# Row sums of a 16384 x 1024 array: 16-row loads in halves from two DMA queues, three blocks of rows, one store more

## The chip, the cores and the metric

The kernel runs on one core of a Trainium2 chip. The metric is the device time of one execution in microseconds (us). Before the change the median of three runs is 160.99 us (160.79 to 161.18). From here on "us" always means device time or a time in the trace of one profiled execution, counted from the first instruction.

## What is computed

The input x is 32 x 512 x 1024 numbers in f32, 67.11 MB. The output is the sum over the last axis, 32 x 512 numbers in f32:

```python
def reference(x):                      # x: (32, 512, 1024) f32
    return np.sum(x, axis=-1).astype(np.float32)
```

Seen flat, these are 16,384 rows of 1,024 columns (4,096 bytes), each summed to one number. Nothing is used twice, so every byte of x crosses from HBM to the on-chip memory (SBUF) once.

## The kernel before

**Layout.** The rows are spread over the 128 partitions, 128 rows for each. The flat array is cut in two blocks. In the first, `x_a` (BODY = 113 rows per partition), partition p holds 113 consecutive rows, so neighbouring partitions start 113 x 4 KB apart in HBM. In the second, `x_z` (LAST = 15 rows per partition), they start 60 KB apart. A column of results, `res_a` with 113 and `res_z` with 15 numbers per partition, belongs to each block.

**Loads.** All loads go out from SyncE (SP in the profile), on its one DMA queue, from the list `loads` at L133. Each is a DMA over all 128 partitions and takes one contiguous stretch per partition: one row (`lead`, 4,096 bytes per partition); seven loads of 16 rows (65,536 bytes per partition) into three buffers `xt0` to `xt2` in turn; then the last block in pieces of 8, 4 and 2 rows (CUTS = 0, 8, 12, 14) into the next of these buffers; then the last row in two parts of 656 and 368 columns (CUT = 656) into `tail`. The first two loads are moved ahead of the start barrier (EARLY = 2). A load into a buffer in its second or third use waits for the VectorE instruction that read the buffer before (`wait_ge(vec, freed[b - BUFS])`). Such a load is issued some 41 us before it lands, with two others ahead of it, and all loads stand in one line.

**Sums.** VectorE (DVE) sums rows with `tensor_reduce` (L58), one instruction for all the rows of a load. ScalarE (ACT) sums single rows with an activation that accumulates (L69). VectorE alone does the lead row and the first six 16-row loads. Of the seventh, VectorE does 9 rows and ScalarE 7 (ACT_ROWS = 7). Of the 8-row piece each does 4, of the 4-row piece each 2, and of the 2-row piece VectorE one row by an add of its two halves with accumulation (L76) and ScalarE the other. The last row's two parts go through L76 one after the other; the second takes in the sum of the first, and waits on `vec` for it.

**Stores.** SP waits until the first part of the last row has landed and until both engines are done with the first block, and stores `res_a` (L137, 452 bytes per partition). Then it waits for all sums and stores `res_z` (L140, 60 bytes per partition). It then waits for the first store, clears semaphores (L144) and waits for the last store.

Of the kernel before, what the change touches and what calls it, by code (L numbers as in the profile page):

```python
# [6 lines left out]
COPY = mybir.ActivationFunctionType.Copy  # L7
X = mybir.AxisListType.X

LEAD = 1  # L10
G = 16
BODY = LEAD + 7 * G
LAST = 15
BUFS = 3
ACT_ROWS = 7
CUT = 656
CUTS = (0, 8, 12, 14)
EARLY = 2


def row_sums(nc, x: bass.AP, out: bass.AP):
    P = nc.NUM_PARTITIONS
    x_flat = x.flatten_outer_dims()
    R, D = x_flat.shape
    C = R // P
    assert R % P == 0 and C == BODY + LAST
    out_flat = out.rearrange("a (b c) -> (a b c)", c=1)

    def block(r0, n):
        x_b = x_flat[r0 : r0 + P * n].rearrange("(p c) d -> p (c d)", p=P)  # L30
        out_b = out_flat[r0 : r0 + P * n].rearrange("(p c) -> p c", p=P)
        return x_b, out_b

    x_a, out_a = block(0, BODY)
    x_z, out_z = block(P * BODY, LAST)

    def sbuf(name, n):
        return nc.alloc_sbuf_tensor(name, [P, n], F32)

    xt = [sbuf(f"xt{i}", G * D) for i in range(BUFS)]  # L40
    lead = sbuf("lead", LEAD * D)
    tail = sbuf("tail", D + 16)
    pairs = [sbuf(f"pairs{i}", D // 2) for i in range(3)]
    res_a = sbuf("res_a", BODY)
    res_z = sbuf("res_z", LAST)

    names = [f"slot{i}" for i in range(BUFS)] + ["first", "piece0", "piece1", "piece2", "tail0"]
    names += ["tail1", "vec", "act", "early_store", "store"]
    sems = {n: nc.alloc_semaphore(n) for n in names}
    slots = [sems[f"slot{i}"] for i in range(BUFS)]  # L50
    vec, act = sems["vec"], sems["act"]
    numbers = [s.num for s in sems.values()]
    assert numbers == list(range(numbers[0], numbers[0] + len(numbers)))

    count = {"vec": 0, "act": 0}

    def rows_dve(t, j, n, res, c):
        nc.vector.tensor_reduce(  # L58
            out=res[:, c : c + n],
            in_=t[:, j * D : (j + n) * D].rearrange("p (j d) -> p j d", d=D),  # L60
            axis=X,
            op=ADD,
        ).then_inc(vec, 1)
        count["vec"] += 1

    def rows_act(t, j, n, res, c):
        for i in range(n):
            v = t[:, (j + i) * D : (j + i + 1) * D]
            nc.scalar.activation(  # L69
                out=v, in_=v, func=COPY, accum_out=res[:, c + i : c + i + 1]  # L70
            ).then_inc(act, 1)
            count["act"] += 1

    def pairs_dve(t, a, b, acc, pairs):
        h = (a + b) // 2
        nc.vector.tensor_tensor_reduce(  # L76
            out=pairs[:, 0 : h - a], in0=t[:, a:h], in1=t[:, h:b], scale=1.0, scalar=0.0,
            op0=ADD, op1=ADD, accum_out=acc,
        ).then_inc(vec, 1)
        count["vec"] += 1  # L80

    n_bufs = (BODY - LEAD) // G


    freed = {}
    loads = [(0, lead[:, :], x_a[:, 0 : LEAD * D], sems["first"])]
    for b in range(n_bufs):
        c = LEAD + b * G
        loads.append((b, xt[b % BUFS][:, :], x_a[:, c * D : (c + G) * D], slots[b % BUFS]))
    last = xt[n_bufs % BUFS]  # L90
    for k, (i, j) in enumerate(zip(CUTS, CUTS[1:])):
        loads.append((n_bufs, last[:, i * D : j * D], x_z[:, i * D : j * D], sems[f"piece{k}"]))
    for k, (i, j, gap) in enumerate(((0, CUT, 0), (CUT, D, 16))):
        e = (LAST - 1) * D
        loads.append((0, tail[:, i + gap : j + gap], x_z[:, e + i : e + j], sems[f"tail{k}"]))


    nc.vector.memset(tail[:, CUT + 15 : CUT + 16], 0.0).then_inc(vec, 1)  # L98
    count["vec"] += 1
    nc.vector.wait_ge(sems["first"], 16)  # L100
    rows_dve(lead, 0, LEAD, res_a, 0)
    for b in range(n_bufs):
        a = ACT_ROWS if b == n_bufs - 1 else 0
        nc.vector.wait_ge(slots[b % BUFS], 16 * (b // BUFS + 1))
        rows_dve(xt[b % BUFS], 0, G - a, res_a, LEAD + b * G)
        freed[b] = count["vec"]
        if a:
            nc.scalar.wait_ge(slots[b % BUFS], 16 * (b // BUFS + 1))
            rows_act(xt[b % BUFS], G - a, a, res_a, LEAD + b * G + G - a)
    body_vec, body_act = count["vec"], count["act"]  # L110

    for k in range(2):
        i, j = CUTS[k], CUTS[k + 1]
        h = (j - i) // 2
        nc.vector.wait_ge(sems[f"piece{k}"], 16)
        rows_dve(last, i, h, res_z, i)
        nc.scalar.wait_ge(sems[f"piece{k}"], 16)
        rows_act(last, i + h, j - i - h, res_z, i + h)
    nc.scalar.wait_ge(sems["piece2"], 16)
    rows_act(last, 13, 1, res_z, 13)  # L120
    nc.vector.wait_ge(sems["piece2"], 16)
    pairs_dve(last, 12 * D, 13 * D, res_z[:, 12:13], pairs[2])
    nc.vector.wait_ge(sems["tail0"], 16)
    pairs_dve(tail, 0, CUT, tail[:, CUT + 14 : CUT + 15], pairs[0])
    nc.vector.wait_ge(sems["tail1"], 16)
    nc.vector.wait_ge(vec, count["vec"])  # L126
    pairs_dve(tail, CUT + 14, D + 16, res_z[:, 14:15], pairs[1])


    for b, dst, src, s in loads:  # L130
        if b >= BUFS:
            nc.sync.wait_ge(vec, freed[b - BUFS])
        nc.sync.dma_start(out=dst, in_=src).then_inc(s, 16)  # L133
    nc.sync.wait_ge(sems["tail0"], 16)
    nc.sync.wait_ge(vec, body_vec)
    nc.sync.wait_ge(act, body_act)
    nc.sync.dma_start(out=out_a, in_=res_a[:, :]).then_inc(sems["early_store"], 16)  # L137
    nc.sync.wait_ge(vec, count["vec"])
    nc.sync.wait_ge(act, count["act"])
    nc.sync.dma_start(out=out_z, in_=res_z[:, :]).then_inc(sems["store"], 16)  # L140


    nc.sync.wait_ge(sems["early_store"], 16)
    nc.sync.sem_clear(range(numbers[0], sems["store"].num))  # L144
    nc.sync.wait_ge(sems["store"], 16).then_inc(sems["store"], -16)


def kernel(tc: tile.TileContext, x: bass.AP, out: bass.AP):
    tc.close()
    tc.compile()  # L150
    nc = tc.nc
    row_sums(nc, x, out)

    sp = mybir.EngineType.SP
    fn = nc.m.functions[0]
    entry, body = None, None
    for blk in fn.blocks:
        ops = [i for i in blk.instructions if i.engine == sp]  # L160
        if entry is None:
            entry = blk
        elif any(i.opcode == "DMACopy" for i in ops):
            body = blk
            break
    code = list(body.instructions)
    loads = [i for i in code if i.engine == sp and i.opcode == "DMACopy"][:EARLY]
    for load in loads:
        assert not load.sync_info.on_wait
        code.remove(load)  # L170
    body.instructions = code
    code = list(entry.instructions)
    at = next(k for k, i in enumerate(code) if i.engine == sp and i.opcode == "Drain")
    code[at:at] = loads
    entry.instructions = code
# [29 lines left out]
```

## Time and profile before

The profile is that of one execution. Times in its rows are in us from the first instruction; "idle before <-releaser" is the time that an engine stood idle ahead of an instruction and what ended it.

| | before |
|---|---|
| time, median of 3 runs | 160.99 us (160.79 to 161.18) |
| span of the profiled execution, first to last instruction | 159.7 us |
| what the median has beyond that span | 1.3 us |
| VectorE busy | 122.6 us (77%), 17 instructions |
| ScalarE busy | 16.3 us (10%), 29 instructions |
| DMA queue of SP | 2160 packets, 67.18 MB, 97.8% of 16 engines' span |
| a 16-row reduce on VectorE | 17,222 ns |
| a row on ScalarE | 1,041 ns, then 187 ns to read the accumulator |

The trace also holds each packet that a DMA engine moved: its start, its time and its size. A packet here is one partition's stretch of one load. Each of the 16 engines moves 8 of them per load, one after the other, and then a 4-byte packet that raises the semaphore (9 ns):

| bytes | of | packets | median time | starts of the first and the last, us |
|---|---|---|---|---|
| 4,096 | lead row | 128 | 159 ns | 1.02, 2.91 |
| 65,536 | 16 rows | 896 | 2,420 ns | 2.65, 136.22 |
| 32,768 | 8 rows | 128 | 1,213 ns | 138.14, 147.10 |
| 16,384 | 4 rows | 128 | 611 ns | 147.82, 152.57 |
| 8,192 | 2 rows | 128 | 309 ns | 152.69, 155.33 |
| 2,624 | 656 columns | 128 | 105 ns | 155.15, 156.35 |
| 1,472 | 368 columns | 128 | 62 ns | 155.97, 156.87 |
| 452 | store of `res_a` | 128 | 26 ns | 157.81, 158.13 |
| 60 | store of `res_z` | 128 | 11 ns | 158.86, 159.05 |

A load has landed when the slowest of its 16 engines has raised the semaphore. The last landings, by the semaphore records, are at 139.02 (the seventh 16-row load), 148.73, 153.62, 156.11, 156.95 and 157.37 us (second part of the last row).

### The profile page before, as it was taken

To read this page: it belongs to the slowest core of one execution; us is meant where nothing else is said; L and a number is where in the kernel's file an instruction comes from. 1 tells how busy PE (TensorE), PEld (TensorE's weight loads), DVE (VectorE), ACT (ScalarE), POOL (GpSimd) and SP (SyncE) were. 2 spreads that over 40 slices of the span, in tenths; PEclk is the share of its full clock that TensorE was granted. 3 is DMA by queue.
4 is the path that set the end of the run, shared out by engine and by line. 5 is a ranking of instruction groups with operands and counts; after the bars stand their busy time and mean duration, and the time that the engine had idled before them with its cause. 6 is when DMAs were issued, how large, how long until landed. Compare 5 with 4: busy or idle time off the path is not lost.

```text
span 159.7 us, 105 instructions
## 1 busy us (share of the span) xinstructions
DVE 122.6 (77%) x17; ACT 16.3 (10%) x29; POOL 0.2 (0%) x4
## 2 busy tenths in 40 slices
DVE  1100029999499985999779996899949999499984
ACT  3000000000000000000000000000000000196783
POOL 0000000000000000000000000000000000000000
DMA  9969969979799699699699699699796996999993
GB/s 394 525 263 525 509 279 525 460 328 525 328 460 525 263 525 525 263 525 525 263 525 509 279 525 492 295 525 443 345 525 295 492 525 295 476 410 394 435 394 107
DMA packets 2160, 67.18 MB, mean 421 GB/s; under 512 B 496, under 2 KB 624, under 8 KB 880
## 3 DMA queue, kind: packets, MB, share of 16 engines
q1 hardware_dynamic: 2160, 67.18, 97.8%
HBM read 67.11 MB, written 0.07 MB: 421 GB/s over the span
## 4 chain that ended last, share of the span: by engine, by line
DMA 75%; DVE 22%; SPq 1%; issue 0%; DVEq 0%
DMA xt<-in_x_dram 51%; DMA tail<-in_x_dram 24%; DVE res_a L58 22%; SPq L133 1%; DVE pairs L76 1%; DVEq L126 0%; DVE tail L76 0%; DVE res_z L76 0%
## 5 line engine op out<-in xcount | busy, mean ns | idle before, releaser
L58 DVE TENSOR_REDUCE res_a<-xt 128x16 f32<-128x16384 f32 (+1 forms) x7 | 113.1, 16155 | 31.0 <-DMA xt<-in_x_dram 31.0
L69 ACT ACTIVATE xt<-xt 128x1024 f32<-128x1024 f32 x14 | 14.6, 1045 | 139.1 <-DMA xt<-in_x_dram 139.1
L58 DVE TENSOR_REDUCE res_z<-xt 128x4 f32<-128x4096 f32 (+1 forms) x2 | 6.7, 3352 | 0.5 <-DMA xt<-in_x_dram 0.5
L69 ACT ACTIVATION_READ_ACCUMULATOR xt<-xt 128x1 f32 x14 | 2.6, 187 | 0.0
L58 DVE TENSOR_REDUCE res_a<-lead 128x1 f32<-128x1024 f32 x1 | 1.2, 1219 | 1.4 <-DMA lead<-in_x_dram 1.4
L98 DVE MEMSET tail<- 128x1 f32 x1 | 0.1, 59 | 2.0 <-PEq L150 2.0
L69 ACT ACT_TABLE_LOAD x1 | 1.3, 1283 | 1.9 <-PEq L150 1.9
L76 DVE CUSTOM_DVE_ANT_0 pairs<-tail 128x328 f32<-128x328 f32 (+1 forms) x2 | 0.9, 427 | 0.3
L76 DVE CUSTOM_DVE_ANT_0 pairs<-xt 128x512 f32<-128x512 f32 x1 | 0.7, 693 | 0.2 <-DMA xt<-in_x_dram 0.2
L76 DVE DVE_READ_ACCUMULATOR2_ANT res_z<- 128x1 f32 x2 | 0.2, 83 | 0.0
L189 POOL MEMSET const-uint8-127<- 128x1 uint8 x1 | 0.1, 102 | 0.0
L189 POOL MEMSET const-bfloat16-1.0<- 128x1 bf16 x1 | 0.1, 101 | 0.0
L189 POOL MEMSET const-float32-0.0<- 128x1 f32 x1 | 0.1, 98 | 0.2 <-issue 0.2
L189 POOL MEMSET const-float32-1.0<- 128x1 f32 x1 | 0.1, 98 | 0.0
L76 DVE DVE_READ_ACCUMULATOR2_ANT tail<- 128x1 f32 x1 | 0.1, 82 | 0.0
## 6 DMA issues: line engine op xcount, KB each, us to landing
xt<-in_x_dram SPq DMA_DIRECT2D x1, 4096.0 KB, 31.2
xt<-in_x_dram SPq DMA_DIRECT2D x1, 2048.0 KB, 35.7
xt<-in_x_dram SPq DMA_DIRECT2D x1, 1024.0 KB, 37.7
lead<-in_x_dram SPq DMA_DIRECT2D x1, 512.0 KB, 3.4
tail<-in_x_dram SPq DMA_DIRECT2D x1, 328.0 KB, 38.0
tail<-in_x_dram SPq DMA_DIRECT2D x1, 184.0 KB, 37.9
xt<-in_x_dram SPq DMA_DIRECT2D x7, 40.8
out_dram<-res_a SPq DMA_DIRECT2D x1, 56.5 KB, 1.6
```

Source lines behind the costliest of these rows:

```text
L58: nc.vector.tensor_reduce(out=res[:, c : c + n], in_=t[:, j * D : (j + n) * D].rearrange("p (j d) -> p j d", d=D), axis=X, op=ADD,).then_i ...
L69: nc.scalar.activation(out=v, in_=v, func=COPY, accum_out=res[:, c + i : c + i + 1]).then_inc(act, 1)
L76: nc.vector.tensor_tensor_reduce(out=pairs[:, 0 : h - a], in0=t[:, a:h], in1=t[:, h:b], scale=1.0, scalar=0.0, op0=ADD, op1=ADD, accum_out ...
L98: nc.vector.memset(tail[:, CUT + 15 : CUT + 16], 0.0).then_inc(vec, 1)
L133: nc.sync.dma_start(out=dst, in_=src).then_inc(s, 16)
L189: nc = _bacc.Bacc("TRN2", target_bir_lowering=False, num_devices=1)
```

## The change

- The rows are cut into three blocks of 32, 48 and 48 rows per partition (BLOCKS). Neighbouring partitions start 128 KB apart in the first and 192 KB apart in the others. All groups are now 16 rows; there are eight. The lead row is row 0 of the first group, in the same buffer.
- Group 0 is loaded by SP as 1 row and 15 rows. Groups 1 to 6 are loaded in two halves of 8 rows (32,768 bytes per partition): rows 0 to 7 from SP's queue, rows 8 to 15 from ScalarE's queue. Both halves raise the same semaphore, and the sums wait for 32 in place of 16. ScalarE issues nothing until group 0 has landed (`wait_ge(slots[0], full[0])`), then issues its six loads, each with the same wait for a free buffer as SP's.
- The last group is loaded by SP in pieces of 9, 4 and 2 rows (CUTS = 0, 9, 13, 15), and its last row as 544 and 480 columns (CUT = 544). ScalarE takes 5 rows of the 9-row piece, VectorE 4.
- ScalarE's loads stand ahead of all its sums in its order, and the load of its function table stands behind them.
- The early stores are three (128, 192 and 128 bytes per partition), issued one after the other at L169 of the changed kernel, once the 2-row piece has landed and the first seven groups are summed. The last store is 16 columns (64 bytes per partition, 192 bytes apart).

The core of the diff:

```diff
+BLOCKS = (32, 48, 48)
-CUT = 656
-CUTS = (0, 8, 12, 14)
+CUT = 544
+CUTS = (0, 9, 13, 15)
...
+    loads = [(0, xt[0][:, 0:D], x_0[:, 0:D], sems["first"], nc.sync)]
+    loads.append((0, xt[0][:, D : G * D], x_0[:, D : G * D], slots[0], nc.sync))
+    full = {0: 16}
+    for b in range(1, n_groups - 1):
+        x_b, _, c = groups[b]
+        for h, issuer in ((0, nc.sync), (1, nc.scalar)):
+            i, j = h * G // 2 * D, (h + 1) * G // 2 * D
+            dst, src = xt[b % BUFS][:, i:j], x_b[:, c * D + i : c * D + j]
+            loads.append((b, dst, src, slots[b % BUFS], issuer))
+        full[b] = (full[b - BUFS] if b >= BUFS else 0) + 32
...
+    def issue(queue):
+        if queue is nc.scalar:
+            queue.wait_ge(slots[0], full[0])
+        for b, dst, src, s, issuer in loads:
+            if issuer is queue:
+                if b >= BUFS:
+                    queue.wait_ge(vec, freed[b - BUFS])
+                queue.dma_start(out=dst, in_=src).then_inc(s, 16)
...
-    nc.sync.wait_ge(sems["tail0"], 16)
+    nc.sync.wait_ge(sems["piece2"], 16)
     nc.sync.wait_ge(vec, body_vec)
     nc.sync.wait_ge(act, body_act)
-    nc.sync.dma_start(out=out_a, in_=res_a[:, :]).then_inc(sems["early_store"], 16)
+    for k, (out_b, res, n) in enumerate(stores):
+        m = n - G if k == len(stores) - 1 else n
+        nc.sync.dma_start(out=out_b[:, 0:m], in_=res[:, 0:m]).then_inc(sems[f"early{k}"], 16)
...
-    nc.sync.dma_start(out=out_z, in_=res_z[:, :]).then_inc(sems["store"], 16)
+    nc.sync.dma_start(out=out_z[:, c_z : c_z + G], in_=res_z[:, c_z : c_z + G]).then_inc(sems["store"], 16)
```

## The prediction

> **What bounds the kernel now.** I read the page first, then the chain of waits, then the timeline's end, then the packets. The page's head:
>
> ```profile
> span 159.7 us, 105 instructions
> ...
> DMA  9969969979799699699699699699796996999993
> ...
> q1 hardware_dynamic: 2160, 67.18, 97.8%
> HBM read 67.11 MB, written 0.07 MB: 421 GB/s over the span
> ```
>
> The reader sees DMA engines that are busy 97.8% of the span, and in the 40 slices none empty from the first to the last. VectorE is busy 77%. The chain of waits, summed by line, says the same: 74.6% of the span is DMA, and the 21.6% of VectorE are links in which the next load waits for a free buffer, not gaps in the stream.
>
> ```profile
> by line: DMA xt<-in_x_dram 50.8%; DMA tail<-in_x_dram 23.8%; DVE res_a L58 21.6%; SPq L133 0.8%; DVE pairs L76 0.5%; issue 0.3%; DVEq L126 0.0%; DVE tail L76 0.0%; DVE res_z L76 0.0%
> ```
>
> The timeline from 100 us on shows the pace and what follows it (columns: start, duration, engine, line, operation, tiles, idle before):
>
> ```profile
> 3.46 1.22 DVE L58 TENSOR_REDUCE res_a<-lead 128x1 f32<-128x1024 f32 x1 [1.41 <-DMA lead<-in_x_dram]
> ...
> 119.69 17.22 DVE L58 TENSOR_REDUCE res_a<-xt 128x16 f32<-128x16384 f32 x1 [2.15 <-DMA xt<-in_x_dram]
> 139.04 9.75 DVE L58 TENSOR_REDUCE res_a<-xt 128x9 f32<-128x9216 f32 x1 [2.13 <-DMA xt<-in_x_dram]
> ...
> 148.75 4.42 DVE L58 TENSOR_REDUCE res_z<-xt 128x4 f32<-128x4096 f32 x1
> ...
> 153.65 2.29 DVE L58 TENSOR_REDUCE res_z<-xt 128x2 f32<-128x2048 f32 x1 [0.47 <-DMA xt<-in_x_dram]
> ...
> 156.14 0.69 DVE L76 CUSTOM_DVE_ANT_0 pairs<-xt 128x512 f32<-128x512 f32 x1 [0.20 <-DMA xt<-in_x_dram]
> ...
> 156.97 0.50 DVE L76 CUSTOM_DVE_ANT_0 pairs<-tail 128x328 f32<-128x328 f32 x1
> ...
> 157.63 0.35 DVE L76 CUSTOM_DVE_ANT_0 pairs<-tail 128x185 f32<-128x185 f32 x1
> ...
> 158.02 0.34 SPq L140 DMA_DIRECT2D out_dram<-res_z  x1
> ```
>
> VectorE starts a 16-row group every 19.35 us (119.69 to 139.04), works 17.22 and waits 2.1 for the next landing. At the end it has little to spare: 0.47 us ahead of the 4-row piece's rows, 0.20 ahead of the 2-row piece's, none ahead of the first part of the last row, whose landing (156.95) and whose free engine (156.14 + 0.69) meet within 0.1 us. From there to the end runs a fixed chain: 156.97 to 157.63 the first part and its wait, 0.36 the second, the store at 158.02, and 1.67 to the end at 159.69.
>
> **The stream, packet by packet.** 16 rows are 8 packets of 2.420 us and a 9 ns semaphore per engine: 19.37, and the groups do land 19.35 apart. 8 rows are 8 x 1.213 + 0.009 = 9.713; the 8-row piece landed 148.73 - 139.02 = 9.71 after the group before it. So packets run without gaps, and the whole time is their sum. Two 32 KB packets cost 2.426 where one of 64 KB costs 2.420: about 6 ns belong to each packet, and (1.213 - 0.006) / 32 KB = 37.7 ns to each KB.
>
> **The change, part by part.**
>
> *Same start.* The lead row lands at about 3.44 as before. The next load has 15 rows, 60 KB per packet: 37.7 x 60 + 6 = 2.269 us, eight and a semaphore 18.16. Group 0 lands at 21.60.
>
> *Halves.* Twelve loads of 8 rows: 12 x 9.713 = 116.56, if packets of two queues follow each other as those of one do. The trace has only one queue, so the price of changing queues is bounded: below by the 6 ns per packet that a second queue could hide, above by the shortest packet in the trace, 11 ns (the 60-byte store). I take zero, as the 6 ns are there already. With 96 such packets per engine the ends are -0.58 and +1.06 us. The stream has then delivered groups 0 to 6 at 138.16.
>
> *Pieces.* 9 rows: 8 x (37.7 x 36 + 6 ns) + 0.009 = 10.92, to 149.08. 4 rows: 8 x 0.611 + 0.009 = 4.90, to 153.98. 2 rows: 2.48, to 156.46. The parts of the last row took 0.84 (656 columns) and 0.42 (368) from landing to landing; in proportion 544 take 0.68 and 480 take 0.58: 157.13 and 157.71. The last byte thus lands 0.34 us later than before (157.37); this is 48 more packets per engine at 6 ns and 6 more semaphores at 9.
>
> *ScalarE's wait and the order of packets.* ScalarE issues only when group 0 has landed, and behind that wait stand all its loads. SP's first half of group 1 has been queued since about 2 us and runs on meanwhile. By the stores, packets start 0.85 us after the issue (156.96 to 157.81; 158.02 to 158.86), so ScalarE's first packets come to the engines at 21.62 + 0.85 = 22.5 or a little later. The engines' last packets of a group end 0.4 to 0.9 us ahead of its landing (138.14 to 138.64 against 139.02), so SP's next two packets run from about 20.7-21.2 to 23.1-23.6, and ScalarE's first comes third. If they alternate from there, each group's last packet lies behind one packet of SP's next load: a lag of one packet, 1.21 us (1.36 for group 6, behind one of 36 KB). Group 6 lands at 139.5, not at 138.16. Neither queue runs dry: a group's loads go out when VectorE has freed the buffer, with a whole group still ahead of them.
>
> *VectorE at the end.* From 139.54: 9.75 to 149.29 (9-row piece landed at 149.08), 4.42 to 153.71, waits for 153.98, 2.29 to 156.29, waits for 156.46. So the lag is covered, with 0.27 + 0.20 to spare: up to a lag of about 1.8 us it costs nothing, beyond that its full size. The row of L76 starts at 156.49, ends 0.69 later at 157.18, so the first part starts at 157.20 (landed 157.13). It is 272 wide in place of 328; the slope between 328 and 185 wide is (500 - 354) / 143 = 1.02 ns, so 0.44, and with the same 0.16 to the next start 157.80 (second part landed 157.71). 241 in place of 185 wide: 0.36 + 0.06. Sums end at 158.22 against 157.99. **Sum: +0.23 us.**
>
> *ScalarE.* 7 rows from 139.54 to 146.9; 5 rows from 149.1 to 154.4; 2 rows (2.19 in the trace) to 156.6; 1 row (1.15) to 157.75. Within 158.22: nothing, with 0.47 of cover. Its function table (1.28 us) moves behind its loads, to about 100 us, into an idle engine: nothing.
>
> *Stores.* SP issues three stores of 0.35 us from 156.5 to 157.6, ahead of the last one's 158.25; the early store took 1.6 us to land, so they land before 159.3, and the end at 159.92 does not wait. The last store has 64 bytes per partition in place of 60: the same 1.67. If the three came late, each would cost its 0.35.
>
> Span 159.69 + 0.23 = 159.92. The median has 1.3 us beyond the span, and I leave that as it is: **161.2 us**, +0.14%. A measurement of this kernel can tell about 0.2% from no change, so anything from 160.67 to 161.31 is the same.
>
> **The rivals.**
>
> *A longer lag (slower).* If ScalarE's first packets come behind three or more of SP's (a slower first issue on that queue, or packets fetched ahead), the lag is two packets, 2.43, and for group 6 with two 36 KB packets 2.73. VectorE then starts group 6 at 140.91 and works without a pause: 9.75, 4.42 and 2.29 bring it to 157.37, and it starts the row of L76 there in place of 156.49. That is 0.88 on top of 0.23, 162.1 us; each further packet adds 1.2 or more. It decides from 1.8 us of lag. For it: VectorE's spare 0.47 and 0.20 us. Against: ScalarE has 0.6 to 1.1 us before SP's third packet. The Trainium skill ("DMA: Bandwidth & Descriptors", section on queues, rings and completion order) says that an engine turns to the next queue only after a whole packet, which it puts at typically 9 to 17 descriptors. A half is 8 data packets and a semaphore in this trace; were that one such packet, the halves would alternate whole, the lag would be zero and this rival out, with the time as forecast. No run here shows it. Chance 0.14.
>
> *Dearer packets in the new layout (slower).* The stride between partitions becomes 128 and 192 KB. The two strides in the trace, 452 and 60 KB, show the same 37 ns per KB, so stride has not mattered, but both are odd multiples of 4 KB. Each 1% on the first block's 38.7 us costs 0.39; the dearest per KB among the loads' packets of a row or more is the 4 KB one (159 ns, 5% over), which would make 2.0. With the price of changing queues this gives 161.5 to 163.2, most likely its lower half, around 162. The skill's same page (section on latency and other measured facts) has copies at 207 GB/s with a stride of 512 KiB against 214 with one padded by 4 KiB; an estimate from it is 3% on the first block, some 1.3 us. No stride of this trace tests it. Chance 0.22.
>
> *Two queues hide the packets' fixed part (faster).* While one queue closes a packet the other's runs: 96 x 6 ns and 12 x 9 ns, 0.68 us off the forecast, 160.5 us. For it: the fixed part is there in the packets. Against: at 2.420 us per 64 KB the 16 engines move 433 GB/s, and without the fixed part it would be 434, a stream that has nowhere shown more. Chance 0.12.
>
> **How the numbers follow.** The forecast has 0.52. Its own range is 161.0 to 161.5: of its 0.52, 0.14 lies above 161.31. Slower: 0.14 + 0.14 + 0.20 of the dearer packets = 0.48. Faster: 0.10 of the hiding queue. The same: the rest, 0.42. The range takes in the faster rival, the longer lag, and the lower half of the dearer packets: 160.5 to 162.4.
>
> **What would show it.** In the changed profile: two queues with equal packets of about 1.213 us; group 1's sums starting near 42.2 (lag one packet), 41.0 (none) or 43.4 (two); groups 19.43 us apart; the sums of group 6 starting near 139.5; idle time before the 4-row and 2-row pieces of about 0.3 and 0.2 us; the last store near 158.25. Groups further apart than 19.5 us mean dearer packets, and closer than 19.4 hidden ones; no idle time before the two pieces, with a start of group 6 after 140, means the longer lag.

## The result, and the profile after

The changed kernel takes 163.00 us (median of 4 runs, 162.91 to 163.94) against 161.03 (4 runs, 160.79 to 161.18): a ratio of 1.0143, with a 95% interval of 1.0125 to 1.0161. The forecast was 161.2 in a range of 160.5 to 162.4. The kernel became slower by 2.0 us, and the time lies outside the range. Each ratio in this document leaves out executions more than 1.5% above the fastest of the same kernel; that is one below, of 164.44 us.

The page of the changed kernel, the lines that answer to those of before (q1 is SyncE's queue, q10 ScalarE's):

```profile
span 161.7 us, 116 instructions
...
DMA  9996999999999999999999999999999999999980
...
q1 hardware_dynamic: 2448, 42.01, 60.9%
q10 hardware_dynamic: 864, 25.17, 36.1%
HBM read 67.11 MB, written 0.07 MB: 415 GB/s over the span
```

The two queues together are busy 97.0% of 161.7 us, 156.9 us, where one queue was busy 97.8% of 159.7, 156.2 us. The reader sees that the transfers themselves have hardly grown. What is new is the end of the row of slices: the last two slices (8 us) are 8 and 0 in tenths where before only the last was low. The chain of waits, summed by line, names what fills that end:

```profile
by line: DMA xt<-in_x_dram 67.1%; DVE res L63 30.7%; DVE pairs L81 0.8%; SPq L145 0.2%; issue 0.2%; DVEq L133 0.0%; DVE tail L81 0.0%; DVE res L81 0.0%
```

The loads of `tail`, 23.8% of the chain before, are gone from it, and VectorE's reduces are 30.7% in place of 21.6%. In the timeline:

```profile
21.72 16.15 DVE L63 TENSOR_REDUCE res<-xt 128x15 f32<-128x15360 f32 x1 [17.06 <-DMA xt<-in_x_dram]
44.79 17.22 DVE L63 TENSOR_REDUCE res<-xt 128x16 f32<-128x16384 f32 x1 [6.92 <-DMA xt<-in_x_dram]
64.22 17.22 DVE L63 TENSOR_REDUCE res<-xt 128x16 f32<-128x16384 f32 x1 [2.20 <-DMA xt<-in_x_dram]
...
122.52 17.22 DVE L63 TENSOR_REDUCE res<-xt 128x16 f32<-128x16384 f32 x1 [2.21 <-DMA xt<-in_x_dram]
...
142.40 16.27 DVE L63 TENSOR_REDUCE res<-xt 128x9 f32<-128x9216 f32 x3 [2.66 <-DMA xt<-in_x_dram]
...
158.58 0.68 DVE L81 CUSTOM_DVE_ANT_0 pairs<-xt 128x512 f32<-128x512 f32 x1
...
160.28 0.33 SPq L173 DMA_DIRECT2D out_dram<-res  x1
```

Group 0 is there at 21.72, as worked out. Group 1 comes 23.07 us later, not 19.4, and from then on the groups are 19.43 apart: the delay is made once, between groups 0 and 1, and kept. The line at 142.40 has three reduces in one ("x3": 9, 4 and 2 rows) and no idle time between them, and the row of L76 (L81 in the changed kernel) follows with no wait. Before, VectorE waited 0.47 and 0.20 us for transfers here. So from 142.40 on nothing but VectorE's own work sets the end: 17.80 us to the end of its sums at 160.20.

The transfers were done long before. By the semaphore records the 9-row piece landed at 149.19, the 4-row piece at 154.09, the 2-row piece at 156.59 and the last part of the last row at 157.84 us, each within 0.15 us of what the prediction had (149.08, 153.98, 156.46, 157.71).

The packets of one DMA engine between 18 and 44 us show where the delay comes from (start in us, S for SyncE's queue, A for ScalarE's, KB; "sem" is the 4-byte packet that raises a semaphore). The trace does not name the engine of a packet: they are joined where the end of one meets the start of the next.

```
18.58 S 60 | 20.85 S sem | 20.85 S 32 | 22.06 S 32 | 23.29 S 32 | 24.50 S 32 | 25.70 A 32 | 26.91 S 32 | 28.12 A 32 | 29.33 S 32
...
35.38 A 32 | 36.59 S sem | 36.60 A 32 | 37.80 S 32 | 39.10 A 32 | 40.31 S 32 | 41.52 A 32 | 42.73 S 32 | 43.94 A sem
```

ScalarE issued at 21.71. Four of SyncE's packets go first, not two; then the queues take turns, one packet each, and the 4-byte packet takes a turn as well. ScalarE's last packet of each group, the one that raises its semaphore, thus lies behind three packets of SyncE's next load. That is 3 x 1.21 = 3.64 us for group 1 (44.79 against 41.03 in order, plus 0.1), and for group 6, behind three 36 KB packets, 3 x 1.364 = 4.09 (142.40 against 138.16).

### The profile page after: what moved, and what is told of

Read it like the earlier page. It is cut to its first block, busy times and chain, and to the rows that moved or that the text cites. A ratio compares the mean times of both kernels' runs of the same rounds, so it can differ in the third digit from the quotient of the medians.

```text
span 161.7 us, 116 instructions
## 1 busy us (share of the span) xinstructions
DVE 121.2 (75%) x17; ACT 17.0 (10%) x31; POOL 0.2 (0%) x4
## 4 chain that ended last, share of the span: by engine, by line
DMA 67%; DVE 32%; SPq 0%; issue 0%; DVEq 0%
DMA xt<-in_x_dram 67%; DVE res L63 31%; DVE pairs L81 1%; SPq L145 0%; DVEq L133 0%; DVE tail L81 0%; DVE res L81 0%
## 5 line engine op out<-in xcount | busy, mean ns | idle before, releaser
L63 DVE TENSOR_REDUCE res<-xt 128x16 f32<-128x16384 f32 (+5 forms) x10 | 119.7, 11992 | 36.9 <-DMA xt<-in_x_dram 36.9
L74 ACT ACTIVATE xt<-xt 128x1024 f32<-128x1024 f32 x15 | 15.6, 1041 | 39.8 <-DMA xt<-in_x_dram 39.8
L81 DVE CUSTOM_DVE_ANT_0 pairs<-tail 128x272 f32<-128x272 f32 (+1 forms) x2 | 0.9, 426 | 0.2 <-DVE tail L81 0.2
L81 DVE CUSTOM_DVE_ANT_0 pairs<-xt 128x512 f32<-128x512 f32 x1 | 0.7, 683 | 0.0
L81 DVE DVE_READ_ACCUMULATOR2_ANT res<- 128x1 f32 x2 | 0.2, 84 | 0.0
L81 DVE DVE_READ_ACCUMULATOR2_ANT tail<- 128x1 f32 x1 | 0.1, 85 | 0.0
```

The source lines that it names most:

```text
L63: nc.vector.tensor_reduce(out=res[:, c : c + n], in_=t[:, j * D : (j + n) * D].rearrange("p (j d) -> p j d", d=D), axis=X, op=ADD,).then_i ...
L74: nc.scalar.activation(out=v, in_=v, func=COPY, accum_out=res[:, c + i : c + i + 1]).then_inc(act, 1)
L81: nc.vector.tensor_tensor_reduce(out=pairs[:, 0 : h - a], in0=t[:, a:h], in1=t[:, h:b], scale=1.0, scalar=0.0, op0=ADD, op1=ADD, accum_out ...
```

## The experiments

Theory A: the lag of ScalarE's queue alone makes the time, through VectorE's last sums. Theory B: the layout, the smaller packets or the three stores cost it. All ratios below are against the kernel before, run beside it on the same chip.

**Both halves on one queue.** The edit (cut; the line `issue(nc.scalar)`, with nothing left to issue, goes too):

```diff
-        for h, issuer in ((0, nc.sync), (1, nc.scalar)):
+        for h, issuer in ((0, nc.sync), (1, nc.sync)):
```

> The changed kernel with both halves of each group on SyncE's queue, in order; blocks, cuts and stores stay. Theory A (ScalarE's queue runs three packets behind, group 6 lands 3.6 to 4.1 us late, and VectorE's last sums set the end): group 6's sums start near 138.2 in place of 142.4, VectorE waits again for the 4-row and 2-row pieces, the sums end near 158.2, and the time is 161.0 to 161.2. Theory B (the layout with strides of 128 and 192 KB, the many packets or the three stores cost the 2 us): 162.5 to 163.0, as with the change.

Measured: 161.13 us, ratio 1.0023 (1.0014 to 1.0032). The timeline of this kernel:

```profile
138.29 9.76 DVE L63 TENSOR_REDUCE res<-xt 128x9 f32<-128x9216 f32 x1 [2.21 <-DMA xt<-in_x_dram]
149.19 4.42 DVE L63 TENSOR_REDUCE res<-xt 128x4 f32<-128x4096 f32 x1 [1.15 <-DMA xt<-in_x_dram]
154.10 2.29 DVE L63 TENSOR_REDUCE res<-xt 128x2 f32<-128x2048 f32 x1 [0.49 <-DMA xt<-in_x_dram]
156.60 0.69 DVE L81 CUSTOM_DVE_ANT_0 pairs<-xt 128x512 f32<-128x512 f32 x1 [0.21 <-DMA xt<-in_x_dram]
```

The waits ahead of the three pieces (1.15, 0.49 and 0.21 us) are back, and the time is near the 161.2 of the prediction. Blocks, cuts, packets of 32 KB and stores are all still in, so theory B falls.

**One row more for ScalarE.** The edit is `ACT_ROWS = 8` in place of 7.

> The changed kernel with 8 rows of group 6 on ScalarE in place of 7, so VectorE sums 8 in place of 9. Theory A: VectorE has no wait from 142.4 to the end, so its end comes one row (1.07 us) earlier, 159.1; ScalarE's last row, at 158.1 before, ends one row (1.04) later, 159.1 too: 1.0 us less, 162.0. Theory B: the end hangs on transfers or stores, no change, 163.0.

Measured: 162.10 us (median of four, 161.90 to 164.44), ratio 1.0076 (1.0060 to 1.0091), 0.7% or 1.1 us under the changed kernel: the gain is the row's 1.07 us. The one profile of this kernel is of the execution of 164.44 us. ScalarE issued at 22.84 in it and group 6's sums started at 144.84, so it does not show the transfers of the other three. But there too VectorE's sums run from group 6 to the end without waiting for a load, for 16.74 us (to 161.58) in place of 17.80, one row less. So the end does hang on VectorE.

**ScalarE's queue used once before.** The edit, in ScalarE's part of `issue` (cut):

```diff
+            queue.dma_start(out=warm[:, :], in_=x_0[:, 0:16]).then_inc(sems["warm"], 16)
             queue.wait_ge(slots[0], full[0])
```

> The changed kernel with one more DMA of 64 bytes per partition, issued by ScalarE on its queue at the start, ahead of its wait for group 0. In the changed kernel the first packet of that queue starts 3.9 us after its issue, behind four packets of SyncE, where stores on SyncE's queue start after 0.85. Theory A1 (a queue's first use is slow): with the queue used once, the first 32 KB packet starts behind two packets of SyncE, the lag is one packet, group 6's sums start near 139.5, and the time is 161.0 to 161.2. Theory A2 (the DMA engines are committed to some two further packets of the queue they work on): still four packets first, group 6 near 142.4, 163.0.

Measured: 163.01 us, ratio 1.0153 (1.0127 to 1.0180). Group 6's sums start as late as with the change:

```profile
142.33 16.27 DVE L64 TENSOR_REDUCE res<-xt 128x9 f32<-128x9216 f32 x3 [2.65 <-DMA xt<-in_x_dram]
```

The first 32 KB packet of ScalarE's queue starts at 25.59, behind four. A slow first use is out. The small load itself shows the same delay: issued at 1.91, its first packet starts at 7.10, behind two packets of group 0, and its other seven per engine then take one turn each behind a 60 KB packet, so that 64 bytes per partition landed at 22.9.

**ScalarE issues at once.** The edit:

```diff
-            queue.wait_ge(slots[0], full[0])
+            queue.wait_ge(sems["first"], 16)
```

> The changed kernel with ScalarE waiting for the lead row (3.4 us) in place of group 0 (21.7 us) before it issues its loads. Theory A, with packets of the two queues in turn: ScalarE's packets come between those of group 0 (8 packets of 2.27 us); behind j of them first, 8 - j packets of 1.21 us get ahead of group 0's last, so groups 0 to 5 land that much later than in order, and group 6 in order at 138.2. For j = 3: group 0 at 27.7, group 5 at 124.7, VectorE free of it at 142.0, and the time 162.6 to 163.0; for j = 1: group 5 at 127, VectorE free at 144.4, 165.3. So it is not faster, though group 6 lands 4 us earlier. If it were only group 6's landing that counted: 161.0 to 161.2. Theory B: 163.0.

Measured: 165.33 us, ratio 1.0281 (1.0267 to 1.0295). That is the figure worked out for j = 1, but the packets show j = 2 on most engines, so the match is partly luck. The timeline:

```profile
30.54 16.15 DVE L63 TENSOR_REDUCE res<-xt 128x15 f32<-128x15360 f32 x1 [25.54 <-DMA xt<-in_x_dram]
...
127.67 33.40 DVE L63 TENSOR_REDUCE res<-xt 128x16 f32<-128x16384 f32 x4 [2.21 <-DMA xt<-in_x_dram]
```

Now group 0 pays: ScalarE's packets get ahead of its own, and it lands near 30.5 in place of 21.7 (3.77 + 18.16 + 7 x 1.213 = 30.4). The first of ScalarE's packets start between 7.3 and 9.7, behind two of group 0's on 13 engines and three on 3. Behind two, six of ScalarE's get ahead of group 0's last packet, as the expectation counts. The seventh gets ahead of the packet that raises group 0's semaphore, a turn that the expectation left out. Group 6 was there early: ScalarE starts its rows of it at 138.60. But VectorE is still summing group 5 (x4 and no idle time from 127.67 on). Turns in packets, in whichever order they begin, move the landing of whole groups.

**The two queues alone, in the kernel before.** The edit (cut):

```diff
-        loads.append((b, xt[b % BUFS][:, :], x_a[:, c * D : (c + G) * D], slots[b % BUFS]))
+        for h in (0, 1):
...
+            i, j = (h * G // 2 * D, (h + 1) * G // 2 * D) if b else (0, G * D)
+            dst, src = xt[b % BUFS][:, i:j], x_a[:, c * D + i : c * D + j]
+            (halves if h else loads).append((b, dst, src, slots[b % BUFS]))
...
+            nc.scalar.wait_ge(slots[0], full[0])
+            for k, dst, src, s in halves:
...
+                nc.scalar.dma_start(out=dst, in_=src).then_inc(s, 16)
```

> The kernel before with one part of the change alone: rows 8 to 15 of its second to seventh 16-row load go out on ScalarE's queue, after the first of these loads has landed (22.7 us). Blocks, cuts and stores stay. Theory A (the lag of ScalarE's queue alone makes the time): four packets of SyncE first, three packets of lag, group 6 near 139.0 + 0.1 + 3.7 = 142.8, no wait of VectorE from there to the 2-row piece, so the sums end some 2.5 us later than at 157.99, and the time is 163.0 to 163.6. Theory B (the new layout has a part in it): at most 161.5.

Measured: 165.38 us, ratio 1.0263 (1.0245 to 1.0281), some 2 us more than expected. The direction is A's, the size is not. The timeline:

```profile
23.23 17.22 DVE L58 TENSOR_REDUCE res_a<-xt 128x16 f32<-128x16384 f32 x1 [18.09 <-DMA xt<-in_x_dram]
47.24 17.22 DVE L58 TENSOR_REDUCE res_a<-xt 128x16 f32<-128x16384 f32 x1 [6.79 <-DMA xt<-in_x_dram]
...
144.38 9.75 DVE L58 TENSOR_REDUCE res_a<-xt 128x9 f32<-128x9216 f32 x1 [2.21 <-DMA xt<-in_x_dram]
```

Group 1 comes 24.01 us after group 0 where 19.4 is in order: a lag of nearly four packets. The packets say why: on 12 engines ScalarE's first starts between 27.05 and 27.73, on the other 4 between 28.30 and 28.67, one of SyncE's packets later, and a load has landed when its slowest engine is done. From 144.38 the sums again take 17.80 us, to 162.18. So the price follows the rule, and the expectation had one packet too few (1.21 us). The rest of the 2 us is a stream that began later in the profiled execution (group 0's sums at 23.23 against 22.76) and a last store that took 1.91 us against 1.67. Why four engines let one packet more go first, the runs do not show.

**Whole loads on one queue, in the new layout.** Groups 1 to 6 go out as single 16-row loads from SyncE (cut):

```diff
-        for h, issuer in ((0, nc.sync), (1, nc.scalar)):
...
+        dst, src = xt[b % BUFS][:, :], x_b[:, c * D : (c + G) * D]
+        loads.append((b, dst, src, slots[b % BUFS], nc.sync))
```

> The changed kernel with groups 1 to 6 loaded whole (16 rows, 64 KB per partition) on SyncE's queue: no halves, no second queue; blocks, cuts and stores as changed. Theory A: 48 packets and 6 semaphores fewer per engine than with halves on one queue, so the stream ends 0.34 us earlier, as before the change; the sums end near 158.0, and the last store, which lands 0.24 us sooner than before the change (1.43 against 1.67), leaves 0.1 to 0.3 us less than before: a ratio of 0.998 to 1.000. Theory B (strides of 128 and 192 KB cost something): a ratio over 1.000.

Measured: 160.97 us, ratio 0.9997 (0.9988 to 1.0007): the time of the kernel before. Its groups stand 19.35 us apart, in the first block and in the others, as they do with strides of 452 KB:

```profile
21.83 16.15 DVE L63 TENSOR_REDUCE res<-xt 128x15 f32<-128x15360 f32 x1 [16.87 <-DMA xt<-in_x_dram]
41.18 17.22 DVE L63 TENSOR_REDUCE res<-xt 128x16 f32<-128x16384 f32 x1 [3.20 <-DMA xt<-in_x_dram]
60.53 17.22 DVE L63 TENSOR_REDUCE res<-xt 128x16 f32<-128x16384 f32 x1 [2.13 <-DMA xt<-in_x_dram]
```

Strides of 128 and 192 KB cost nothing that can be measured. Against the halves on one queue (1.0023) the whole loads save 0.26%, 0.4 us; the count of packets had given 0.34.

**ScalarE issues a little sooner: three doses of the lag.** Group 0's load is cut so that a part of it lands earlier, and ScalarE waits for that part (here 12 rows; the other two runs have 13 and 14). The edit (cut):

```diff
-    loads.append((0, xt[0][:, D : G * D], x_0[:, D : G * D], slots[0], nc.sync))
+    loads.append((0, xt[0][:, D : 13 * D], x_0[:, D : 13 * D], sems["begin"], nc.sync))
+    loads.append((0, xt[0][:, 13 * D : G * D], x_0[:, 13 * D : G * D], slots[0], nc.sync))
...
-            queue.wait_ge(slots[0], full[0])
+            queue.wait_ge(sems["begin"], 16)
```

12 rows:

> The changed kernel with group 0's second load cut in 12 and 3 rows, and ScalarE waiting for the 12 rows (landing near 18.0) in place of the whole group (21.7), so it issues 3.7 us sooner; both queues stay in use. Theory A: its first 32 KB packets come behind at most two of SyncE's in place of four, the lag is one packet or none, group 6 lands at 138.2 to 139.6, VectorE waits for the pieces, and the time is 161.0 to 161.3. If two queues cost by themselves: over 162.

13 rows:

> The changed kernel with group 0's second load cut in 13 and 2 rows and ScalarE waiting for the 13 rows (landing near 19.2). Theory A with a threshold: its first packets come behind two of SyncE's, the lag is one packet, group 6 near 139.6, and VectorE still waits before the 4-row or the 2-row piece, with under 0.5 us left: 161.1 to 161.5, as with no lag. A price for each packet of lag from the first on (0.65 us): 161.7 to 161.9.

14 rows:

> The changed kernel with group 0's second load cut in 14 and 1 rows, and ScalarE waiting for the 14 rows (landing near 20.4), so it issues 1.3 us sooner. Theory A: its first packets come behind three of SyncE's, the lag is two packets, group 6 near 141.0, VectorE's chain without a wait from there ends 1.2 to 1.4 us earlier than with the change, and the time is 161.5 to 161.8: between the change and the kernel with no lag. If the price of a lag has no threshold but is 2.0 / 3 for each packet: 162.3.

| ScalarE waits for | it issues at | its first packet | SyncE's halves ahead | group 6's sums start | ratio to before (95%) |
|---|---|---|---|---|---|
| 12 rows | 18.55 | 22.20 | 1 packet, lag 0 | 139.01 | 1.0023 (1.0013 to 1.0034) |
| 13 rows | 19.52 | 23.38 | 2, lag 1 | 139.93 | 1.0022 (1.0013 to 1.0031) |
| 14 rows | 20.68 | 24.76 | 3, lag 2 | 141.25 | 1.0055 (1.0042 to 1.0068) |
| group 0 (the change) | 21.71 | 25.65 | 4, lag 3 | 142.40 | 1.0143 (1.0125 to 1.0161) |

In microseconds: 161.48, 161.41, 162.01 and 163.00. The run with 14 rows came out 0.2 over what was expected, the run with 12 rows 0.2 over its 161.3 too. In the profiled executions of both, the stream began later (the lead row's sums start at 3.79 and 4.06 against 3.44); that this is the reason is not shown, as it began at 3.82 with 13 rows, whose time was as expected. A lag of one packet costs nothing, two cost 0.3% and three 1.2%, so there is a threshold. The profile with 13 rows shows it:

```profile
139.93 14.08 DVE L63 TENSOR_REDUCE res<-xt 128x9 f32<-128x9216 f32 x2 [2.35 <-DMA xt<-in_x_dram]
154.38 2.29 DVE L63 TENSOR_REDUCE res<-xt 128x2 f32<-128x2048 f32 x1 [0.37 <-DMA xt<-in_x_dram]
156.88 0.69 DVE L81 CUSTOM_DVE_ANT_0 pairs<-xt 128x512 f32<-128x512 f32 x1 [0.21 <-DMA xt<-in_x_dram]
```

VectorE goes from 9 to 4 rows without a pause ("x2") but still waits 0.37 and 0.21 us later on: the lag is used up there. With 14 rows no wait is left ("x3"):

```profile
141.25 16.27 DVE L63 TENSOR_REDUCE res<-xt 128x9 f32<-128x9216 f32 x3 [2.51 <-DMA xt<-in_x_dram]
```

With no lag two queues give 1.0023 and one queue with the same halves gives 1.0023: the second queue by itself neither gains nor costs, within 0.1%.

**The last store by ScalarE.** In the changed kernel the last store is issued on ScalarE's queue, when no load is under way. The edit (cut; the two waits ahead of the store go to ScalarE with it, and SyncE waits for the same sums and the store before it clears the semaphores):

```diff
-    nc.sync.dma_start(out=out_z[:, c_z : c_z + G], in_=res_z[:, c_z : c_z + G]).then_inc(sems["store"], 16)
+    nc.scalar.dma_start(out=out_z[:, c_z : c_z + G], in_=res_z[:, c_z : c_z + G]).then_inc(sems["store"], 16)
```

> The changed kernel with the last store issued by ScalarE, when the DMA engines are idle. If ScalarE's queue takes 3.5 to 4 us from issue to first packet always, the store's packets start 3.5 us or more after the issue and the time is near 166; if the delay comes from the packets of the other queue that the engines are committed to, they start 0.8 to 1.0 us after the issue and the time stays near 163.

Measured, in a single run: 163.55 us. The issue is this line of the timeline:

```profile
160.60 0.35 ACTq L173 DMA_DIRECT2D out_dram<-res  x1
```

Its first packet starts at 161.45, 0.85 us later, just as on SyncE's queue. ScalarE's queue is not slow by itself; beside a stream of the other queue its first packet takes 3.5 us and more.

**The last store with 60 bytes.** In the kernel with whole loads (cut):

```diff
-        m = n - G if k == len(stores) - 1 else n
+        m = n - G + 1 if k == len(stores) - 1 else n
...
-    nc.sync.dma_start(out=out_z[:, c_z : c_z + G], in_=res_z[:, c_z : c_z + G]).then_inc(sems["store"], 16)
+    nc.sync.dma_start(out=out_z[:, c_z + 1 : c_z + G], in_=res_z[:, c_z + 1 : c_z + G]).then_inc(sems["store"], 16)
```

> The kernel with whole loads on one queue and the changed blocks, with the last store cut from 64 to 60 bytes per partition (15 of the 16 columns; the first goes with the third early store, which then waits for VectorE's sums of the 9-row piece as well). If the 60 bytes make the last store of the kernel before slower, it lands 1.6 to 1.9 us after its issue in place of 1.4, and the time is 0.2 to 0.5 us more than with 64 bytes; if the 192 bytes from one partition's stretch to the next make it fast: 1.4 us, no change.

Measured: 161.04 us, ratio 0.9998 (0.9988 to 1.0008); the store landed 1.41 us after its issue (158.11 to 159.53), as with 64 bytes. It is not the 60 bytes that made the store of the kernel before take 1.67 (1.91 in the run of the two queues alone). Those 60-byte pieces lay end to end in HBM, these are 192 bytes apart. The distance may decide, but so may where each piece starts or the other stores ahead; none of these was tried by itself.

## Why the prediction was wrong, point by point

- *Same start, halves, pieces.* Right. Group 0 at 21.72 (21.60), groups 19.43 apart, the last byte at 157.84 (157.71). Changing queues from packet to packet costs nothing that can be measured, and a second queue hides nothing: lag 0 on two queues and halves on one give the same ratio, and groups are 19.43 apart in both. The 11 ns that bounded this price is not the shortest packet, as the one that raises a semaphore takes 9; nothing hung on it.
- *ScalarE's wait and the order of packets.* This step failed, in its third sentence: "By the stores, packets start 0.85 us after the issue". The stores go to idle engines. Beside SyncE's stream ScalarE's first packet took 3.94 us, so four packets went first in place of two, and the lag of group 6 was 4.1 us in place of 1.4. The sums ended at 160.20 in place of 158.22. The rest of the step, turns of one packet each, a lag of one packet less than went first, and a delay that is kept to the end, held in every trace where SyncE's halves went first.
- *VectorE at the end.* The mechanism held: one packet of lag (1.4 us) is covered, two (2.7) are not. The limit is nearer 2.2 us than 1.8: with both halves on one queue group 6's sums start at 138.29 and all sums end at 158.29, and a chain of 17.80 us without a wait that ends there starts at 140.49. The prediction's chain without a wait is 18.19 long (140.91 to 159.10), 0.39 too much; the reduces of 9, 4 and 2 rows, for one, take 16.27 back to back, and not 9.75 + 4.42 + 2.29. Beyond the limit the end follows group 6 one to one: 17.80 us from the start of its sums to the end of all sums, in the changed kernel, with 14 rows and in the kernel before with two queues.
- *The first rival*, the longer lag, was the right one. It had 0.14, and was priced for two packets at 162.1 with "1.2 or more" for each further; three give 163.3, less 0.26 for the quicker last store 163.0, as measured. That it fits so well is partly luck: group 6's sums start 1.49 us after the start with two packets (142.40 against 140.91), 0.29 more than the 1.2, and the chain from there is 0.39 shorter. The range took in this rival with two packets only. The margin named against it, 0.6 to 1.1 us, hung on the same 0.85 us.
- *The Trainium skill on turns.* The Trainium skill ("DMA: Bandwidth & Descriptors", section on queues, rings and completion order) gives turns of a whole packet, typically 9 to 17 descriptors. Had a half been one packet, there would have been no lag; the trace has turns of one 32 KB stretch of one partition, so the measurement decides against that reading here. The same page of the Trainium skill says that issuing from several engines saves the sequencer's time alone (section on issuing engines); the runs agree, with 1.0023 against 1.0023.
- *Dearer packets.* Out: 19.35 us between groups at strides of 128 and 192 KB. The loss that the Trainium skill gives for a stride of 512 KiB (207 GB/s, beside 214 for one of 4 MiB padded by 4 KiB; same page, section on latency and other measured facts) has no counterpart at these strides.
- *ScalarE and the early stores.* Right: ScalarE ended at 158.09 under VectorE's 160.20, and the three stores went out from 156.60 and were not waited for.
- *The last store* was taken at 1.67 us and took 1.41 (160.28 to 161.69): 0.26 us too much.

What stays open is why the first packet comes so late. On most engines what passed ahead of it, beyond the packet under way 0.85 us after the issue, was one packet of 60 KB (ScalarE issues at once), two of 32 KB (the change, 14 rows), two of 32 KB and some of 8 (13 rows), or one of 32 KB and three or four of 12 (12 rows). This fits engines that have already taken in some 50 to 60 KB of the queue they work on. A fixed delay of about 3.4 us whenever the engines are busy fits these runs as well, as both come to the same time at this rate. Neither fits the four engines of the two queues in the kernel before, where three packets of 32 KB passed and ScalarE's first came 5.1 to 5.4 us after the issue. No run here decides.

## What to carry to other kernels

A latency that is read from a transfer on idle engines is not that of a transfer beside a full queue; where the order of two queues hangs on it, bound it by the packets already queued ahead. When a load is split over two queues that take turns, as here, a head start of one queue is kept for the whole kernel, and every split load lands late by it. Such a lag is free as long as the consumer waits anyway, so add up the consumer's idle time from the last late load to the end: here it was 1.85 us (1.15, 0.49 and 0.21, with both halves on one queue), enough for a lag of 1.4 us and not for one of 4.1.

## What the runs showed of the hardware

- Two queues with loads waiting took turns of one packet (one partition's stretch) on each DMA engine, and the 4-byte packet that raises a semaphore took a turn of its own (36.59 and 43.94 us in the changed kernel).
- A load of 64 bytes per partition beside a stream of 60 KB packets got one packet per turn and engine: its packets started at 7.10 us, and it landed at 22.9.
- Beside a full queue the first packet of the second queue started 3.5 to 5.2 us after its issue in these runs, and 0.85 us after it on idle engines.
- Stores of 60 bytes per partition landed 1.67 and 1.91 us after the issue when they lay end to end, and 1.41 when 192 bytes apart.
